# Turning two query tiles per stick-breaking head without TensorE, with weights as differences for B and a late division for A

## The chip, the cores and the metric

The kernel runs on one core of one Trainium2 chip. The metric is the device time of one execution in microseconds (us). The time before the change is 806.25 us, the median of 3 runs (804.82 to 810.35).

## The reference

One encoder layer over 1024 prompt rows and 32 sample rows of width 1024, in float32. Two groups of eight heads read the same normalised input: A is a softmax attention in a band with a clipped relative bias, B is stick-breaking attention (each key takes its share of what the later keys have left over). Both results are gated, projected, normalised and added, and a per-layer embedding is gated in.

```python
u = rmsnorm(h, g_pre) @ w_in
qa, ka, va, ga, qb, kb, vb, gb = jnp.split(u, SPLIT_IDX, axis=-1)
...
def band_attention(q, k, v, q_pos, k_pos, bias_table):
    s = jnp.einsum('bqhd,bkhd->bhqk', q, k).astype(jnp.float32) * ATTN_SCALE
    ...
    s = s + bias_table[:, rel].astype(jnp.float32)[None]
    ...
    s = jnp.where(ok[None, None], s, NEG_INF)
    w = jax.nn.softmax(s, axis=-1).astype(v.dtype)
    return jnp.einsum('bhqk,bkhd->bqhd', w, v)
...
def stick_breaking(q, k, v, q_pos, k_pos):
    z = jnp.einsum('bqhd,bkhd->bhqk', q, k).astype(jnp.float32) * ATTN_SCALE
    causal = (k_pos[None, :] < q_pos[:, None])[None, None]
    log_beta = jax.nn.log_sigmoid(z)
    log_1m = jnp.where(causal, jax.nn.log_sigmoid(-z), 0.0)
    after = lax.cumsum(log_1m, axis=3, reverse=True) - log_1m
    w = jnp.where(causal, jnp.exp(log_beta + after), 0.0).astype(v.dtype)
    return jnp.einsum('bhqk,bkhd->bqhd', w, v)
```

Then y = concat(oA * silu(gA), oB * silu(gB)) @ w_out, h + RMSNorm(y), and the embedding with its gate h @ w_ple_gate.

## The kernel before

**How it is written down.** Every operation is recorded by a planner (`Recorder`, from line 264). Each gets a cost from a table of assumed durations (`cost`, lines 338 to 369) and a key, and `order` (372 to 437) simulates the five engines and the one DMA queue with them and fixes the program that each engine runs, in order: PE (TensorE), DVE (VectorE), ACT (ScalarE), POOL (GpSimd) and SP (SyncE, which issues the DMAs). All instructions are issued at line 450, so rows of the profile all say L450 and are told apart by the names of their tiles. On PE the operations of attention go ahead of the dense products where both are ready; the two are woven at 1252 to 1276. If one cost or one operation changes, the whole order is made anew.

**Numbers.** Products run in fp32r, with each operand split in a part that fp32r holds (`...h`, written by an ACT cast) and the rest (`...l`, by a DVE or POOL subtract): hi x hi, hi x lo and lo x hi are added in PSUM.

**Stages.** First the input rows are normalised and the first products made. Then come eight units, A0, B0, A1, B1, A2, B2, A3, B3 (line 1184), each a pair of heads. Beside the attention of a unit PE makes the dense products of the next unit's q, k and v columns (`col_steps`, from 712: tiles `mm_qA`, `mm_kB` and so on, each chunk of 352 rows 24 matmuls in four parts). Unit 7 has no next one; beside it run all eight gate products, `mm_gA` and `mm_gB`. A gate chunk is the product, a sigmoid on ACT, a multiply on DVE, and a multiply on POOL with the attention result read back from DRAM (tiles `sggA`, `oggA`; scratch `o_dr`); it is stored to `og_dr`. The last two B gates wait for the last attention step. After attention its pools are closed (1407), the output weights come in four rounds (`woB_0` to `woB_3` and `woT_0` to `woT_3`, two raw buffers, tag "ao"), ACT and DVE split them, PE makes the embedding products (`ple`), then the products of the output (`o0P` first; operands `oB` and `A11o`, the first block of gated rows), and of the embedding's gate.

**One head.** Eight query tiles of 128 rows. `begin` (784) loads A's bias. `scores(i)` (813 to 852) makes the scores `SA_i_j` or `SB_i_j` in PSUM, in two halves j where there are over 512 columns. A's tile has up to 5 blocks of 128 keys, B's tile i has i + 1.
- A: DVE adds the bias and takes the row maximum, negates it; ACT takes the exponential with the row sum; DVE takes the reciprocal; POOL scales the tile of weights. The small columns are `statA`.
- B: DVE adds the mask to the diagonal block; ACT writes sigmoid(-z) to `om` and sigmoid(z) to `be`; DVE scans the products of sigmoid(-z) from the right; POOL multiplies the two.

The weights stand in `be`, a ring of 3384 columns, the scratch of scan and bias in `om`, a ring of 3076 (line 514). `weights_t(i)` (860 to 903) turns the tile so that keys are on partitions, into the rings `wTh` and `wTl`. It has two ways. Most tiles go through PE: transposes `ptwA` or `ptwB`, up to four blocks to a PSUM bank, then an ACT cast and a DVE subtract. Tiles named in `ROUND` (line 31: 4 and 6 of A's heads, none of B's) go around PE: DVE turns every 32 x 32 square into `om`, one DMA stores that to a scratch in DRAM (`swapA`), four DMAs bring it back in the right places of `be`, and the ACT cast and the DVE subtract read it there (lines 870 to 895). `values(g)` (910 to 927) makes the products with v for four query tiles, `PVA_g` or `PVB_g`; `otB` is its result on the way to `o_dr`. Both `weights_t` and `values` are put two steps behind the scores (`LAG_T`, `LAG_V`).

Of the kernel before, what the change touches and what calls it, by code (L numbers as in the profile page):

```python
# [30 lines left out]
ROUND = {"A": ((4,),(6,)), "B": ()}  # L31
# [424 lines left out]
def stream_step(  # L456
# [22 lines left out]
    o_dr = [scratch([P, T], f"o_dr{n}") for n in range(8)]  # L479
    og_dr = scratch([8, P, T], "og_dr")  # L480
# [33 lines left out]
    ring0, ring1 = Arena(rec, at, "om", 3076), Arena(rec, at, "be", 3384)  # L514
# [11 lines left out]
    NAMES = ["qA", "kA", "vA", "gA", "qB", "kB", "vB", "gB"]  # L526

# [78 lines left out]
    def bias_rows():  # L606

        rb = ring0.tile([8, 257], "rb")
        dma(rb, rel_bias[0])
        R = ring1.tile([8, 768], "R")  # L610
        nc.gpsimd.memset(R, 0.0)
        nc.vector.tensor_scalar(R[:, 256:768], R[:, 256:768], rb[:, 0:1], None, ALU.add)
        nc.vector.tensor_copy(R[:, 0:256], rb[:, 0:256][:, ::-1])
        dma(r_dr, R)
# [97 lines left out]
    def col_steps(j):  # L712
# [7 lines left out]
        def mms(c, part):  # L720
# [20 lines left out]
            if k == "g":  # L741
# [36 lines left out]
    def attention(ab, p, h):  # L778
# [5 lines left out]
        def begin():  # L784
            if ab == "A":
                bias = at2.tile([P, 640], F32, tag="bias", name=f"bias{nm}", bufs=2)
                dma(bias, bias_src(2 * p + h, P, 0, 640))
                nc.gpsimd.memset(bias[0:HD, 0:HD], NEG)
                nc.gpsimd.memset(bias[HD:P, 576:640], NEG)
                box["bias"] = bias  # L790

# [21 lines left out]
        def scores(i):  # L813
# [14 lines left out]
            if ab == "B":  # L828
# [6 lines left out]
                for a, b, s in pieces:  # L835
                    nc.scalar.activation(w1[:, a:b], s, AF.Sigmoid)
                for a, b, s in reversed(pieces):
                    rev = w0[:, a + 1:b + 1][:, ::-1]
                    nc.vector.tensor_tensor_scan(rev, rev, s, 1.0 if b == n else w0[:, b + 1:b + 2], ALU.mult, ALU.bypass)
                nc.gpsimd.tensor_tensor(w1[:, 0:n], w1[:, 0:n], w0[:, 1:n + 1], ALU.mult)  # L840
            else:
                m = small.tile([P, 4], F32, tag="stat", name=f"stat{nm}_{i}", bufs=6)
                for j, (a, b, s) in enumerate(pieces):
                    nc.vector.tensor_tensor_reduce(
                        w0[:, a:b], s, box["bias"][:, n - b:n - a][:, ::-1], 1.0,
                        -3e38 if j == 0 else m[:, j - 1:j], ALU.add, ALU.max, m[:, j:j + 1])
                last = len(pieces) - 1
                nc.vector.tensor_scalar(m[:, 2:3], m[:, last:last + 1], -1.0, None, ALU.mult)
# [1002 lines left out]
```

## Time and profile before

| | |
|---|---|
| median of 3 runs | 806.25 us (804.82 to 810.35) |
| span of the profiled execution | 802.6 us; the page gives no other time of that execution |
| granted TensorE clock | 0.999 |
| instructions | PE 4734 matmuls, DVE 1129, ACT 1163, POOL 554 |
| TensorE's waits for other engines, over 0.1 us | 4.9 us in 8 rows |
| DMA | 145.39 MB in the main queue, 61.3% of its engines' time |

The span runs from the first instruction to the last. A row of an operation reads: line, engine, operation, output and inputs by tile name, shape, count, busy time, mean ns of one, and the idle time of that engine just before it with what ended it. A matmul's own duration is longer than the time it holds up the next one, since they are pipelined.

### The profile page before, as it was taken

To read this page: it belongs to the slowest core of one execution; us is meant where nothing else is said; L and a number is where in the kernel's file an instruction comes from. 1 tells how busy PE (TensorE), PEld (TensorE's weight loads), DVE (VectorE), ACT (ScalarE), POOL (GpSimd) and SP (SyncE) were. 2 spreads that over 40 slices of the span, in tenths; PEclk is the share of its full clock that TensorE was granted. 3 is DMA by queue.
4 is the path that set the end of the run, shared out by engine and by line. 5 is a ranking of instruction groups with operands and counts; after the bars stand their busy time and mean duration, and the time that the engine had idled before them with its cause. 6 is when DMAs were issued, how large, how long until landed. Compare 5 with 4: busy or idle time off the path is not lost.

```text
span 802.6 us, 14554 instructions
## 1 busy us (share of the span) xinstructions
PE 792.0 (99%) x4734; PEld 731.4 (91%) x4734; DVE 565.7 (70%) x1129; ACT 539.5 (67%) x1163; POOL 469.5 (58%) x554
## 2 busy tenths in 40 slices
PE   9999999999999999999999999999999999999997
PEld 7899999999999999999999899999998877888786
DVE  7627878777787888776787586854554786587655
ACT  6636787786586777776787577644437868876741
POOL 6625867795686866635473265554553448599613
PEclk9999999999999999999999999999999999999999
DMA  9419986538876565833325656344389957769634
GB/s 293 135 46 285 236 230 186 153 112 254 220 229 198 145 184 158 208 103 102 92 60 141 146 158 205 99 149 138 105 277 300 288 174 242 236 197 345 215 117 131
DMA packets 147390, 146.32 MB, mean 182 GB/s; under 512 B 37409, under 2 KB 109257, under 8 KB 147314
## 3 DMA queue, kind: packets, MB, share of 16 engines
q1 hardware_dynamic: 147314, 145.39, 61.3%
q8 instruction: 38, 0.62, 0.3%
q14 instruction: 38, 0.31, 0.1%
HBM read 90.78 MB, written 46.16 MB: 171 GB/s over the span
## 4 chain that ended last, share of the span: by engine, by line
PE 89%; DVE 3%; DMA 2%; POOL 2%; ACT 1%; issue 1%; SPq 1%; POOLq 0%; DVEq 0%; ACTq 0%
PE mm_gB L450 6%; PE mm_gA L450 6%; PE mm_kB L450 6%; PE mm_qB L450 6%; PE mm_qA L450 5%; PE mm_kA L450 5%; PE mm_vB L450 4%; PE PVB L450 4%; PE mm_vA L450 4%; PE SB L450 4%; PE ptwB L450 4%; PE SA L450 3%; PE PVA L450 3%; PE g0P L450 2%; PE g1P L450 2%; PE o1P L450 2%
## 5 line engine op out<-in xcount | busy, mean ns | idle before, releaser
L450 POOL TENSOR_TENSOR be<-be,om 128x512 f32<-128x512 f32 (+8 forms) x66 | 82.9, 1260 | 77.8 <-DVE om L450 43.9
L450 DVE TENSOR_TENSOR_SCAN om<-om,SB 128x384 f32<-128x384 f32 (+5 forms) x96 | 92.6, 968 | 21.9 <-ACT be L450 11.7
L450 POOL TENSOR_SCALAR be<-be,statA 128x640 f32<-128x640 f32 (+3 forms) x64 | 44.4, 698 | 44.4 <-DVE statA L450 35.8
L450 DVE TENSOR_TENSOR wTl<-ptwB,wTh 128x512 fp32r<-128x512 f32 (+3 forms) x96 | 50.8, 546 | 13.8 <-ACT wTh L450 12.4
L450 ACT ACTIVATE om<-SB 128x384 f32<-128x384 f32 (+5 forms) x96 | 47.4, 499 | 19.0 <-DVE SB L450 14.2
L450 ACT CAST wTh<-ptwB 128x512 fp32r<-128x512 f32 (+3 forms) x96 | 44.6, 483 | 14.5 <-PE ptwB L450 10.5
L450 ACT ACTIVATE be<-om,statA 128x640 f32<-128x640 f32 (+3 forms) x64 | 44.6, 698 | 11.2 <-DVE statA L450 9.6
L450 ACT ACTIVATE be<-SB 128x384 f32<-128x384 f32 (+5 forms) x96 | 46.8, 498 | 6.8 <-DVE om L450 6.3
L450 PE MATMUL ptwB<-ident,be 128*128 128x128 f32 x288 | 44.0, 273 | 0.1
L450 PEld LDWEIGHTS ptwB<-ident,be 128*128 128x128 f32 x288 | 34.9, 140 | 2.2 <-PE mm_vA L450 0.4
L450 DVE CUSTOM_DVE_ANT_0 om<-SA,biasA 128x320 f32<-128x320 f32 (+2 forms) x64 | 30.7, 480 | 5.3 <-PE SA L450 4.9
L450 PE MATMUL SB<-kdB,LB 128*128 128x384 f32 (+5 forms) x96 | 34.0, 357 | 0.3 <-DVE om L450 0.3
L450 ACT CAST wTh<-ptwA 128x512 fp32r<-128x512 f32 (+2 forms) x64 | 26.0, 429 | 12.0 <-PE ptwA L450 11.4
L450 DVE TENSOR_TENSOR wTl<-ptwA,wTh 128x512 fp32r<-128x512 f32 (+2 forms) x64 | 29.7, 482 | 4.9 <-ACT wTh L450 4.0
L450 PE MATMUL SB<-klB,LB 128*128 128x384 f32 (+5 forms) x96 | 32.9, 347 | 0.0
L450 PE MATMUL SA<-kdA,LA 128*128 128x320 f32 (+2 forms) x96 | 30.0, 319 | 1.1 <-DVE LA L450 0.8
L450 PE MATMUL SA<-klA,LA 128*128 128x320 f32 (+2 forms) x96 | 29.8, 319 | 0.0
L450 POOL TENSOR_TENSOR gB<-gB,gB 128x256 f32<-128x256 f32 x32 | 26.6, 848 | 0.7 <-DMA gB<-in_w_ple_gate_dram 0.4
L450 PE MATMUL ptwA<-ident,be 128*128 128x128 f32 x160 | 26.5, 274 | 0.0
L450 DVE TENSOR_TENSOR SB<-SB,maskb 128x128 f32<-128x128 f32 x64 | 18.0, 292 | 9.9 <-PE SB L450 8.0
L450 POOL TENSOR_TENSOR oB<-oB,oB 128x256 f32<-128x256 f32 x32 | 23.6, 754 | 1.4 <-DMA oB<-in_w_out_dram 1.3
L450 POOL TENSOR_TENSOR h<-h,x 128x512 f32<-128x512 f32 (+1 forms) x18 | 23.0, 1295 | 0.8 <-DVE h L450 0.8
(706 smaller groups left out, 2668.3 us busy)
## 6 DMA issues: line engine op xcount, KB each, us to landing
swapA<-om SPq DMA_DIRECT2D x16, 320.0 KB, 3.5
be<-swapA SPq DMA_DIRECT2D x64, 80.0 KB, 2.9
oB<-in_w_out_dram SPq DMA_DIRECT2D x16, 256.0 KB, 3.9
sum_dro<-oB SPq DMA_DIRECT2D x16, 256.0 KB, 2.9
gB<-in_w_ple_gate_dram SPq DMA_DIRECT2D x16, 256.0 KB, 3.7
sum_drg<-gB SPq DMA_DIRECT2D x16, 256.0 KB, 3.2
x<-in_x_prompt_dram SPq DMA_DIRECT2D x16, 256.0 KB, 4.1
h_dr<-h SPq DMA_DIRECT2D x8, 512.0 KB, 3.6
```

The costliest lines, as they stand in the source:

```text
L450: getattr(getattr(tc.nc, o.what[0]), o.what[1])(*args, **kw)
```

## The change

Three things are done together.

1. `ROUND` names tiles 4 and 6 of B's heads too, so these go through DVE squares and DRAM. That takes 96 `ptwB` transposes off PE, with 32 ACT casts and 32 DVE subtracts of up to 512 columns behind them, and puts in 16 DVE turns, 16 stores `swapB`, 64 loads, and 16 casts and 16 subtracts of 640 and 896 columns.
2. B's weights become differences. With r(j) the product of sigmoid(-z) over the keys from j on, the weight of key j is r(j + 1) - r(j). So the second sigmoid goes (96 ACT instructions), the scan runs in place, and POOL subtracts where it multiplied.
3. A divides late. Its weights stay unscaled; the sums of a head's eight tiles go to one tile `sums`, whose reciprocals (one per head) PE transposes and a DMA stores to `rs_dr`. Each A gate chunk reads those rows back, spread over 64 partitions by two DMAs, and POOL multiplies once more with them. 64 POOL scalings of up to 640 columns go and 12 multiplies of 352 come; 64 small DVE reciprocals become 8. The scores are made negative (query scale, bias, mask and the row minimum in place of the maximum), so that the 64 small DVE negations go too.

The ring `be` shrinks from 3384 to 3328 columns. In all PE has 4646 matmuls in place of 4734, SP issues 781 DMAs in place of 668, and ACT loads its function table 12 times in place of 8.

```diff
-ROUND = {"A": ((4,),(6,)), "B": ()}
+ROUND = {"A": ((4,),(6,)), "B": ((4,),(6,))}
...
+    rs_dr = scratch([8, T], "rs_dr")
...
-    ring0, ring1 = Arena(rec, at, "om", 3076), Arena(rec, at, "be", 3384)
+    ring0, ring1 = Arena(rec, at, "om", 3076), Arena(rec, at, "be", 3328)
...
+    def fixed_columns():
+        x = small.tile([8, NS], F32, tag="fixed", name="fixed")
+        nc.gpsimd.memset(x, 1.0)
+        dma(rs_dr[:, SEQ:T], x)
...
-                box["og"] = at2.tile([P, CH], F32, tag="bias", name=f"og{kind}{p}_{c}", bufs=2)
-                dma(box["og"], o_dr[n][:, cs])
+                box["og"] = at2.tile([P, 2, CH], F32, tag="stg", name=f"og{kind}{p}_{c}", bufs=3)
+                dma(box["og"][:, 0], o_dr[n][:, cs])
+                if ab == "A":
+                    for h in range(2):
+                        row = rs_dr.real[2 * p + h:2 * p + h + 1, cs]
+                        dma(box["og"][h * HD:(h + 1) * HD, 1], Raw(rs_dr, bass.AP(tensor=row.tensor, offset=row.offset, ap=[[0, HD], [1, CH]])))
...
-                nc.gpsimd.tensor_tensor(sg, sg, box["og"], ALU.mult)
+                nc.gpsimd.tensor_tensor(sg, sg, box["og"][:, 0], ALU.mult)
+                if ab == "A":
+                    nc.gpsimd.tensor_tensor(sg, sg, box["og"][:, 1], ALU.mult)
...
-                nc.scalar.activation(box["st"][:, cs], acc, AF.Copy, scale=SCALE)
+                nc.scalar.activation(box["st"][:, cs], acc, AF.Copy, scale=-SCALE if ab == "A" else SCALE)
...
+                box["sums"] = small.tile([P, 8], F32, tag="sums", name=f"sums{nm}", bufs=2)
...
-                for a, b, s in pieces:
-                    nc.scalar.activation(w1[:, a:b], s, AF.Sigmoid)
                 for a, b, s in reversed(pieces):
-                    rev = w0[:, a + 1:b + 1][:, ::-1]
-                    nc.vector.tensor_tensor_scan(rev, rev, s, 1.0 if b == n else w0[:, b + 1:b + 2], ALU.mult, ALU.bypass)
-                nc.gpsimd.tensor_tensor(w1[:, 0:n], w1[:, 0:n], w0[:, 1:n + 1], ALU.mult)
+                    rev = w0[:, a:b][:, ::-1]
+                    nc.vector.tensor_tensor_scan(rev, rev, s, w0[:, b:b + 1], ALU.mult, ALU.bypass)
+                nc.gpsimd.tensor_tensor(w1[:, 0:n], w0[:, 1:n + 1], w0[:, 0:n], ALU.subtract)
...
-                nc.vector.tensor_scalar(m[:, 2:3], m[:, last:last + 1], -1.0, None, ALU.mult)
-                nc.scalar.activation(w1[:, 0:n], w0[:, 0:n], AF.Exp, bias=m[:, 2:3], accum_out=m[:, 3:4])
-                nc.vector.reciprocal(m[:, 3:4], m[:, 3:4])
-                nc.gpsimd.tensor_scalar(w1[:, 0:n], w1[:, 0:n], m[:, 3:4], 1.0, ALU.mult, ALU.mult)
+                nc.scalar.activation(w1[:, 0:n], w0[:, 0:n], AF.Exp, bias=m[:, last:last + 1], scale=-1.0, accum_out=sums[:, i:i + 1])
+                if i == 7:
+                    nc.vector.reciprocal(sums, sums)
+                    pt = psum("T", f"pts{nm}")
+                    nc.tensor.transpose(pt[0:8, 0:P], sums, ident)
+                    row = at.tile([P, 4 * P], F32, tag="ot", name=f"sumrow{nm}", bufs=2)[0:8, 0:P]
+                    nc.scalar.copy(row, pt[0:8, 0:P])
+                    dma(rs_dr[2 * p + h, 0:SEQ].rearrange("(i q) -> i q", q=P), row)
```

How it moves instructions is seen best in the first B head. On PE, before, the transposes of tile 6 stand between the dense products of q (a number behind a name is one buffer of that name):

```order
L450 MATMUL SB_3_0_1905<-kdB_1302,LB_1306 128x512
L450 MATMUL SB_3_0_1905<-klB_1305,LB_1306 128x512
L450 MATMUL mm_qA_0_1795<-hnl_126,wh_qA_0_1613 128x352
L450 MATMUL mm_qA_0_1795<-hnl_126,wh_qA_1_1624 128x352 x4
L450 MATMUL ptwB_6_0_1923<-ident,be 128x128 x4
L450 MATMUL ptwB_6_4_1928<-ident,be 128x128 x3
L450 MATMUL mm_qA_1_1857<-hnh_124,wh_qA_0_1613 128x352 x4
```

After the change PE's program at the scores of tile 3 of the next head reads so; the transposes of tile 6 are gone, and dense products have moved together:

```order
L450 MATMUL SB_3_0_1834<-kdB_1262,LB_1266 128x512
L450 MATMUL SB_3_0_1834<-klB_1265,LB_1266 128x512
L450 MATMUL mm_kA_2_1737<-hnl_145,wh_kA_1_1337 128x352 x4
L450 MATMUL mm_qA_0_1799<-hnh_140,wh_qA_0_1602 128x352 x4
L450 MATMUL mm_qA_0_1799<-hnh_140,wh_qA_1_1615 128x352
L450 MATMUL SB_4_0_1864<-kdB_1262,LB_1266 128x320
L450 MATMUL SB_4_0_1864<-klB_1265,LB_1266 128x320
```

Further on PE the product with v of this head's last four tiles stands before:

```order
L450 MATMUL mm_qA_1_1857<-hnl_127,wh_qA_0_1613 128x352 x4
L450 MATMUL SB_4_1_1996<-kdB_1302,LB_1306 128x320
L450 MATMUL SB_4_1_1996<-klB_1305,LB_1306 128x320
L450 MATMUL mm_qA_1_1857<-hnl_127,wh_qA_1_1624 128x352
L450 MATMUL PVB_1_1893<-wTh,v2B_1417 128x512 x4
L450 MATMUL SB_5_0_2009<-kdB_1302,LB_1306 128x384
L450 MATMUL SB_5_0_2009<-klB_1305,LB_1306 128x384
```

and after. It needs the turned tile 6, now out of `be` and not out of PSUM; the number of matmuls since tile 6's scores (`SB_6_1_1699`) is 138:

```order
L450 MATMUL SB_5_0_1955<-klB_1265,LB_1266 128x384
L450 MATMUL mm_qA_1_1886<-hnh_141,wl_qA_1_1595 128x352 x2
L450 MATMUL mm_qA_1_1886<-hnl_144,wh_qA_0_1602 128x352 x4
L450 MATMUL mm_qA_1_1886<-hnl_144,wh_qA_1_1615 128x352 x4
L450 MATMUL PVB_1_1881<-wTh,v2B_1408 128x512 x4
L450 MATMUL SB_5_1_1983<-kdB_1262,LB_1266 128x384
L450 MATMUL SB_5_1_1983<-klB_1265,LB_1266 128x384
```

On DVE, before, tile 6 is two subtracts out of PSUM, which stand among the masks and scans of the next head:

```order
L450 TENSOR_TENSOR wTl<-ptwB_5_4_1900,wTh 128x256
L450 TENSOR_TENSOR SB_1_0_1841<-SB_1_0_1841,maskb 128x128
L450 TENSOR_TENSOR SB_2_0_1845<-SB_2_0_1845,maskb 128x128
L450 TENSOR_TENSOR SB_3_0_1905<-SB_3_0_1905,maskb 128x128
L450 TENSOR_TENSOR wTl<-ptwB_6_0_1923,wTh 128x512
L450 TENSOR_TENSOR wTl<-ptwB_6_4_1928,wTh 128x384
L450 SCALAR_TENSOR_TENSOR om<-om,SB_1_0_1841 128x256
L450 SCALAR_TENSOR_TENSOR om<-om,SB_2_0_1845 128x384
L450 SCALAR_TENSOR_TENSOR om<-om,SB_3_0_1905 128x512
L450 TENSOR_TENSOR wTl<-ptwB_7_0_1974,wTh 128x512
```

After the change DVE turns tile 6 (the first row) and goes on with other work:

```order
L450 STREAM_TRANSPOSE om<-be 128x7x4x32
L450 SCALAR_TENSOR_TENSOR om<-om,SB_7_1_1754 128x512
L450 SCALAR_TENSOR_TENSOR om<-om,SB_7_0_1700 128x512
L450 TENSOR_TENSOR v2B_1408<-vtB_1386,v2B_1408 128x8x64
L450 SCALAR_TENSOR_TENSOR om<-om,SB_0_0_1755 128x128
L450 TENSOR_TENSOR SB_1_0_1820<-SB_1_0_1820,maskb 128x128
L450 TENSOR_TENSOR SB_2_0_1821<-SB_2_0_1821,maskb 128x128
L450 TENSOR_TENSOR v2B_1687<-vtB_1386,v2B_1687 128x8x64
L450 SCALAR_TENSOR_TENSOR om<-om,SB_1_0_1820 128x256
L450 TENSOR_TENSOR SB_3_0_1834<-SB_3_0_1834,maskb 128x128
L450 TENSOR_TENSOR otB_0_1583<-PVB_0_1707,otB_0_1583 64x512
```

and the subtract of tile 6 is the last but one row of what follows; 20 instructions lie between the turn and the subtract:

```order
L450 TENSOR_TENSOR wTl<-ptwB_5_0_1679,wTh 128x512
L450 TENSOR_TENSOR wTl<-ptwB_5_4_1715,wTh 128x256
L450 STREAM_TRANSPOSE ktA_1711<-stkA_1348 128x512
L450 TENSOR_TENSOR wTl<-be,wTh 128x4x5x32
L450 SCALAR_TENSOR_TENSOR om<-om,SB_2_0_1821 128x384
L450 TENSOR_TENSOR wTl<-ptwB_7_0_1898,wTh 128x512
L450 SCALAR_TENSOR_TENSOR om<-om,SB_3_0_1834 128x512
L450 TENSOR_TENSOR SB_4_1_1931<-SB_4_1_1931,maskb 128x128
L450 SCALAR_TENSOR_TENSOR om<-om,SB_4_1_1931 128x320
L450 SCALAR_TENSOR_TENSOR om<-om,SB_4_0_1864 128x320
L450 TENSOR_TENSOR wTl<-be,wTh 128x4x7x32
L450 TENSOR_TENSOR SB_5_1_1983<-SB_5_1_1983,maskb 128x128
```

On SP, before, the same stretch holds loads and stores of weight sums and of finished rows:

```order
L450 DMA oB_1764<-in_w_out_dram 128x512
L450 DMA oB_1772<-in_w_out_dram 128x512
L450 DMA out_dram<-vtB_1382 128x8x128
L450 DMA sum_dro<-oB_1764 128x512
L450 DMA oB_1836<-in_w_out_dram 128x512
L450 DMA kdA_1793<-kdA_1793 64x1024
L450 DMA o_dr_67<-otB_0_1595 64x512
L450 DMA oB_1907<-in_w_out_dram 128x512
L450 DMA klA_1797<-klA_1797 64x1024
L450 DMA out_dram<-ktA_1730 32x16x32 x4
```

After the change the stores and loads of the squares stand among them, tile 6's last load behind the store of `otB_0`:

```order
L450 DMA be<-swapB_4_104 32x4x160 x2
L450 DMA oB_1760<-in_w_out_dram 128x512
L450 DMA oB_1761<-in_w_out_dram 128x512
L450 DMA be<-swapB_4_104 32x4x160 x2
L450 DMA swapB_6_105<-om 128x896
L450 DMA oB_1804<-in_w_out_dram 128x512
L450 DMA out_dram<-vtB_1386 128x8x128
L450 DMA be<-swapB_6_105 32x4x224 x3
L450 DMA o_dr_67<-otB_0_1583 64x512
L450 DMA sum_dro<-oB_1761 128x512
L450 DMA be<-swapB_6_105 32x4x224
```

Where attention ends, ACT before splits the last round of output weights and casts the first block of gated rows, `A11o`, with several `ple` copies still to come:

```order
L450 CAST oB_7524<-woB_3_7772 128x512
L450 CAST oB_7525<-woB_3_7772 128x512
L450 COPY ple_1_7754<-ple_1_7822 128x512
L450 CAST php_6519<-ptp_7466 128x2x32
L450 CAST A11o_7863<-uo_6588 128x512
L450 CAST oT_7527<-woT_3_7810 128x512
L450 COPY ple_0_7661<-ple_0_7832 128x512
L450 CAST oT_7526<-woT_3_7810 128x512
L450 COPY ple_1_7818<-ple_1_7841 128x512
```

After the change all but one of the `ple` copies are ahead of it, and the last round of weights comes right before it:

```order
L450 COPY xA11o_7626<-uo_7540 128x512
L450 CAST whA11o_7392<-uo_7540 128x512
L450 CAST oB_7359<-woB_3_7598 128x512
L450 CAST oB_7360<-woB_3_7598 128x512
L450 COPY ple_0_7677<-ple_0_7634 32x512
L450 CAST A11o_7683<-uo_6367 128x512
L450 CAST oT_7362<-woT_3_7623 128x512
L450 COPY xA12o_7694<-uo_6367 128x512
```

More of the change, by code (lines that the diff above doesn't have):

```diff
@@ L611, in bias_rows @@
         nc.gpsimd.memset(R, 0.0)
-        nc.vector.tensor_scalar(R[:, 256:768], R[:, 256:768], rb[:, 0:1], None, ALU.add)
-        nc.vector.tensor_copy(R[:, 0:256], rb[:, 0:256][:, ::-1])
+        nc.vector.tensor_scalar(R[:, 256:768], R[:, 256:768], rb[:, 0:1], None, ALU.subtract)
+        nc.vector.tensor_scalar(R[:, 0:256], rb[:, 0:256][:, ::-1], -1.0, None, ALU.mult)
         dma(r_dr, R)
@@ L1017, in scores @@
                         w0[:, a0:b0], s, bx["bias"][:, NK - b0:NK - a0][:, ::-1], 1.0,
-                        -3e38 if j == 0 else m[:, 0:1], ALU.add, ALU.max, m[:, j:j + 1])
-                nc.vector.tensor_scalar(m[:, 2:3], m[:, 1:2], -1.0, None, ALU.mult)
-                nc.scalar.activation(w1[:, 0:NK], w0[:, 0:NK], AF.Exp, bias=m[:, 2:3], accum_out=m[:, 3:4])
+                        3e38 if j == 0 else m[:, 0:1], ALU.add, ALU.min, m[:, j:j + 1])
+                nc.scalar.activation(w1[:, 0:NK], w0[:, 0:NK], AF.Exp, bias=m[:, 1:2], scale=-1.0, accum_out=m[:, 3:4])
                 nc.vector.reciprocal(m[:, 3:4], m[:, 3:4])
```

8 lines of the change are left out of this document (5 added, 3 removed).

## The prediction

> **What bounds the kernel now.** I read the page's busy line and chain first, then the busy time by stretches, then the waits of TensorE (PE).
>
> ```profile
> PE 792.0 (99%) x4734; PEld 731.4 (91%) x4734; DVE 565.7 (70%) x1129; ACT 539.5 (67%) x1163; POOL 469.5 (58%) x554
> ...
> PE 89%; DVE 3%; DMA 2%; POOL 2%; ACT 1%; issue 1%; SPq 1%; POOLq 0%; DVEq 0%; ACTq 0%
> ```
>
> PE is busy in 792.0 of 802.6 us and holds 89% of the chain. The stretches say whether that is so where the change works: from about 70 to 576 us, the attention.
>
> ```profile
> 40.00:600.00 560.00, 557.59 (x3611) 540.05 (x3610) 404.48 (x874) 377.61 (x839) 332.65 (x402) 1.00 0.59 165
> ...
> 120.00:130.00 10.00, 10.00 (x67) 9.63 (x66) 8.96 (x12) 7.58 (x18) 9.18 (x13) 1.00 0.57 185
> ...
> 300.00:390.00 90.00, 90.00 (x585) 87.67 (x585) 70.15 (x163) 68.08 (x147) 51.93 (x67) 1.00 0.56 148
> ```
>
> The columns are length, then busy time of PE, PEld, DVE, ACT and POOL, the granted clock, the DMA share and GB/s. Between 40 and 600 us PE idles for 2.4 us of 560, at a clock of 1.00, with 557.59 / 3611 = 0.154 us for a matmul. Over 90 us of that VectorE (DVE) is at 78%; over ten of them at 90%. So PE work that goes here shortens the kernel one for one, work saved on the others does nothing by itself, and the engine that could take over is DVE.
>
> ```profile
> PE idle L450 <- DVE newh L450: 1.3, 1, 1.3
> ...
> PE SA L450 <- DVE LA L450: 0.8, 1, 0.8
> ...
> PE SB L450 <- DVE om L450: 0.3, 1, 0.3
> PE PVA L450 <- ACT wTh L450: 0.2, 1, 0.2
> ```
>
> Of these waits the last two are the whole price that A's existing turned tiles and a full score ring have today: 0.5 us.
>
> **The change part by part.** *The PE transposes of B.* Tile 4 has 5 blocks and tile 6 has 7, so 12 of a head's 36 transposes go, 96 in all.
>
> ```profile
> L450 PE MATMUL ptwB<-ident,be 128*128 128x128 f32 x288 | 44.0, 273 | 0.1
> ...
> 127.20 1.05 PE L450 MATMUL ptwB<-ident,be 128*128 128x128 f32 x8
> ```
>
> The first row gives 273 ns from start to end of one, but matmuls overlap. The second row, eight in one block that lasts 1.05 us, shows what one holds up the next by: (1.05 - 0.273) / 7 = 0.111 us. The busy column gives 44.0 / 288 = 0.153, which has latency in it wherever a short run ends. I take 0.111: 96 x 0.111 = 10.7 us gone, with 96 x 0.153 = 14.7 as the far end. A's late division adds one transpose of the row sums per head, 8 x 0.111 = 0.9. Net: -9.8 us. The Trainium skill ("TensorE: Matmul & The Clock Gate", Part 4: PE-mode transpose) gives about 275 ns for a transpose inside a kernel; as a latency it agrees with the 273 of the row, as a price the block of eight speaks against it, and by it the sum would be about 24 us instead of 9.8.
>
> *The way that takes their place.* A's tiles 4 and 6 have gone it all along:
>
> ```profile
> L450 DVE STREAM_TRANSPOSE om<-be 128x640 f32<-128x640 f32 x16 | 13.4, 838 | 3.1 <-POOL be L450 3.1
> ...
> L450 ACT CAST wTh<-be 128x640 fp32r<-128x640 f32 x16 | 11.6, 727 | 0.7 <-DMA be<-swapA 0.6
> ...
> L450 DVE TENSOR_TENSOR wTl<-be,wTh 128x640 fp32r<-128x640 f32 x16 | 18.1, 1131 | 4.6 <-ACT wTh L450 4.2
> ...
> swapA<-om SPq DMA_DIRECT2D x16, 320.0 KB, 3.5
> be<-swapA SPq DMA_DIRECT2D x64, 80.0 KB, 2.9
> ```
>
> The last column of the DMA rows is the time from issue to landing. B's tile 6 has 896 columns, 1.4 times 640. Along the path after its scores, from these rows and the next: the diagonal mask 0.29, a sigmoid 0.55, two scans 2.22, the POOL subtract 1.77, the turn 0.838 x 1.4 = 1.17, the store 3.5, four loads about 4.2 (three further issues of some 0.4, then 2.9), the cast 0.727 x 1.4 = 1.02, the subtract 1.131 x 1.4 = 1.58: 16.3 us without queues.
>
> ```profile
> L450 DVE TENSOR_TENSOR_SCAN om<-om,SB 128x448 f32<-128x448 f32 x16 | 17.8, 1112 | 4.5 <-ACT be L450 2.2 <-ACT om L450 2.0
> ...
> L450 POOL TENSOR_TENSOR be<-be,om 128x896 f32<-128x896 f32 x8 | 14.2, 1773 | 15.2 <-DVE om L450 12.5 <-ACT Kh0sA L450 1.9 <-ACT be L450 0.8
> ...
> L450 DVE TENSOR_TENSOR SB<-SB,maskb 128x128 f32<-128x128 f32 x64 | 18.0, 292 | 9.9 <-PE SB L450 8.0 <-PE ptwB L450 1.4
> ...
> L450 DVE TENSOR_TENSOR wTl<-ptwB,wTh 128x512 fp32r<-128x512 f32 x48 | 32.4, 681 | 12.1 <-ACT wTh L450 11.1 <-PE PVB L450 0.6
> ...
> L450 ACT ACTIVATE om<-SB 128x448 f32<-128x448 f32 x16 | 8.8, 551 | 6.1 <-DVE SB L450 3.4 <-PE SB L450 2.3 <-POOL be L450 0.3
> ```
>
> What time has it? In the changed order of the first B head, 138 matmuls stand between the last scores of tile 6 and PVB_1's first product: 138 x 0.154 = 21.3 us; the shortest of the eight heads has 133, the others 151 to 283. The 5 us left are for queues. The store and loads share SP's queue: the fourth load of tile 6 is behind the store of otB_0, which waits for the PVB_0 products, so everything behind that store waits with it. On DVE 20 instructions stand between the turn of tile 6 and its subtract: eight scans (about 7.5 us by the scan groups, 512 columns at 1.24), four masks 1.17, four splits 2.6 and four others 2.6 (estimated at 0.65 each, near the split of 512 columns), 13.9 us. The turn cannot begin before the masks of SB_7_1 and the next head's SB_0_0, which stand 31 matmuls (4.8 us) after the scores. So 4.8 + 0.3 + 1.2 + 13.9 + 1.6 = 21.8 us, and the subtract is wanted eight matmuls after the first product, at 22.5. It fits with 0.7 us to spare: tight, in the engine that is nearest to full. Bounds: nothing, if it always fits (or a gain of the 0.5 us that the two waits above cost); 8 heads x 1.1 = 9 us, if each subtract of tile 6 takes its worst.
>
> ```profile
> L450 DVE TENSOR_TENSOR wTl<-be,wTh x16: 800/826/2494, 94.2 to 488.5; 128x640 fp32r<-128x640 f32 x16
> ```
>
> This is its minimum, median and maximum; 2.494 is 1.7 above the median, less the 0.7 to spare gives about 1.1. I take +0.5, as much again as A's sixteen turned tiles cost now, since A's row is the same mechanism; A had a little more room (158 to 200 matmuls in the five heads where this can be counted alike). The Trainium skill ("SBUF — State Buffer", SBUF: two separate sides) says that a VectorE operation with two SBUF inputs and a GpSimd operation that reads SBUF lock each other out for a whole instruction; the spread 800 to 2494 agrees, and the new subtract, which reads `be` in place of PSUM, puts B's tiles under that rule too.
>
> *Work off PE.*
>
> ```profile
> L450 ACT ACTIVATE be<-SB 128x384 f32<-128x384 f32 (+5 forms) x96 | 46.8, 498 | 6.8 <-DVE om L450 6.3
> ...
> L450 POOL TENSOR_SCALAR be<-be,statA 128x640 f32<-128x640 f32 (+3 forms) x64 | 44.4, 698 | 44.4 <-DVE statA L450 35.8
> ...
> L450 POOL TENSOR_TENSOR sggA<-sggA,oggA 128x352 f32<-128x352 f32 x12 | 11.5, 960 | 11.0 <-DVE sggA L450 9.7 <-issue 1.3
> ...
> L450 DVE RECIPROCAL statA<-statA 128x1 f32<-128x1 f32 x64 | 9.7, 155 | 3.8 <-ACT be L450 3.3
> ...
> L450 DVE TENSOR_SCALAR statA<-statA 128x1 f32<-128x1 f32 x64 | 9.5, 149 | 1.2
> ```
>
> ACT loses the second sigmoids, -46.8; POOL the normalisations, -44.4, and gains 11.5; DVE loses 9.7 + 9.5 in A's units and gains 8 x (0.84 + 1.17) = 16 for the turns in B's, so it is even overall and some 2 us a head fuller where it is fullest. B's subtract on POOL in place of the multiply is the same shape and costs nothing. SP issues 113 more DMAs, and the 12.6 MB of B's squares (12 blocks of 64 KB, out and back, eight heads) raise the queue's 145 MB by 9%. All this costs and brings nothing as long as PE does not wait: it lies beside the 557.59 us. If that cover goes, the price is that of the DVE queue above.
>
> *The end of attention.* PE's dense work of the last unit is spread differently: between the last PVB_0 and the first `o` product now stand 197 matmuls, before 247, so 50 x 0.154 = 7.7 us less cover for loading and splitting the output weights.
>
> ```profile
> 575.07 0.80 PE L450 MATMUL PVB<-wTl,v2B 128*128 128x512 f32 x4
> ...
> 618.30 0.40 PE L450 MATMUL ple<-wph0False,php 128*64 128x512 f32 x1
> ...
> 619.23 1.08 PE L450 MATMUL o0P<-oB,A11o 128*128 128x512 f32 x4
> ```
> ```profile
> 612.72 0.62 ACT L450 CAST A11o<-uo 128x512 fp32r<-128x512 f32 x1
> ```
> ```profile
> 613.37 0.69 DVE L450 TENSOR_TENSOR A11o<-xA11o,A11o 128x512 fp32r<-128x512 f32 x1 [0.54 <-ACT A11o L450]
> ```
>
> A11o was ready at 614.06, 38.2 us after PVB_0's end (575.87), and used at 619.23, 43.4 after it. With 7.7 less it is used at 35.7: 2.5 us late if nothing else moved (upper bound), none if the weights start as much earlier as the order of SP allows. In ACT's order, though, the cast of A11o now stands behind the copy of the next to last PLE group. That group ends where the last begins, at 618.30 in the row above, so copy 0.2 + cast 0.62 + subtract 0.69 follow it while PE has 0.93 us left: +0.6, with a hand-over +0.7, which I take.
>
> **The sum.** 802.6 - 10.7 + 0.9 + 0.5 + 0.7 = 794.0 us of span. The median of the runs, 806.25, stands 3.65 above the profiled span (which is all that the page gives of that execution); with it 797.6 us, 8.6 less or -1.1%. A measurement of this kernel can tell about 1% (8.1 us, so 798.2) from no change: the forecast lies just beyond it.
>
> **The rivals.**
> 1. The turned tiles come late. Place: PVB_1 of each B head, or the ring that its tiles hold longer. For it: 0.7 us to spare on DVE, 90% busy there. Against: A's tiles cost 0.2 us. It decides at 0.7 us of delay per head; 1.2 us of wait in each of the 8 heads eats the whole gain, so 0.5 to 1.5 us gives 801 to 809. It ends slower by 1% where each head waits 2.2 us more (17.9 / 8), which is four DMA landings taking 3 us longer together: 815.
> 2. The end is late by 3 to 6 us, because the last weight round now waits for the last gate store: 600 to 620 us would show PE idle, and the time is 800 to 803.
> 3. PE gains more: at 0.153 us a transpose 88 x 0.153 = 13.5, and with no new wait 806.25 - 13.5 = 792.8. By the 0.273 of the group row as a full price, as the page's rule above would have it, 88 x 0.273 = 24.0 gives 783.5. The block of eight speaks against that.
> 4. Nothing moves, because PE is not the bound: 806. Only where DVE sets the pace in all B units; the 90.00 of 90.00 row speaks against it.
>
> **How the numbers follow.** My forecast, 795.5 to 800: 0.55, of which 0.37 lies below 798.2. Rival 3: 0.15 (0.02 of it the full latency). Rivals 1 and 4 without a loss over 1%: 0.15, with one: 0.08. Rival 2: 0.07. Faster by over 1%: 0.37 + 0.15 = 0.52; within 1%: 0.18 + 0.15 + 0.07 = 0.40; slower: 0.08. The range reaches from rival 3's 793 to 804.5, beyond which rival 1 keeps about 0.13; on the low side 0.04 is left out.
>
> **What would show it.** PE with 4646 matmuls and some 10 us less busy time, its idle time still under 13 us; no row of PE waiting for wTl or wTh in PVB over 1 us in total; one short wait ahead of the o products; POOL and ACT 30 to 45 us less busy. I am wrong if PVB, SB or the transposes left in B wait for DVE by more than a few us, or if PE's busy time falls by much more or less than 10.

## The result and the profile after

The changed kernel takes 807.28 us (median of 20 runs, 806.2 to 809.1), the kernel before 806.27 (20 runs); the ratio is 0.9996 (95% interval 0.9981 to 1.001). That is no change, where 797.6 was forecast. The profiled execution has a span of 806.5 us (before: 802.6). The 20 times of the kernel before lie in two groups, eleven from 804.8 to 806.3 us and nine from 809.1 to 811.1, and by its span its profiled execution is one of the quick ones, so that the two profiles are 3.9 us apart where the medians are 1.0 apart.

The page of the changed kernel, and its time by stretches (length, then busy PE, PEld, DVE, ACT, POOL, granted clock, DMA share, GB/s):

```profile
PE 784.5 (97%) x4646; PEld 722.4 (90%) x4646; DVE 575.5 (71%) x1007; ACT 507.8 (63%) x1063; POOL 436.8 (54%) x503
...
PE 84%; ACT 5%; POOL 3%; DVE 3%; DMA 2%; issue 2%; SPq 1%; DVEq 0%; ACTq 0%; POOLq 0%
```
```profile
0.00:40.00 40.00, 35.51 (x204) 30.89 (x205) 27.41 (x43) 24.91 (x49) 24.18 (x47) 1.00 0.66 215
40.00:600.00 560.00, 550.46 (x3529) 531.84 (x3528) 411.81 (x748) 344.38 (x736) 300.91 (x351) 1.00 0.67 190
600.00:806.50 206.50, 198.55 (x917) 159.62 (x915) 136.25 (x217) 138.50 (x280) 111.71 (x106) 0.98 0.69 224
```

The first and last of these stretches in the kernel before:

```profile
0.00:40.00 40.00, 36.97 (x210) 32.79 (x211) 28.38 (x44) 25.26 (x49) 24.51 (x46) 1.00 0.68 215
...
600.00:802.60 202.60, 197.49 (x917) 158.58 (x915) 132.88 (x212) 136.58 (x275) 112.31 (x107) 1.00 0.69 224
```

TensorE (PE) is busy for 7.5 us less, and idle for 11.4 us more: 22.0 in place of 10.6. Of the idle time 7.1 us are new between 40 and 600 us (9.5 in place of 2.4), 2.8 after 600, 1.5 in the first 40. PE's share of the chain falls from 89 to 84%, and ACT appears in it with 5%. In the waits of PE eight rows of 4.9 us in total have become sixteen; the first of them:

```profile
PE o0P L450 <- ACT A11o L450: 2.5, 1, 2.5
PE ptx L450 <- DVE be L450: 2.2, 2, 1.3
PE SB L450 <- DVE om L450: 1.9, 3, 1.1
PE mm_kB L450 <- ACT stvA L450: 1.5, 1, 1.5
PE PVA L450 <- ACT wTh L450: 1.3, 1, 1.3
PE ptwA L450 <- ACT be L450: 1.3, 1, 1.3
PE idle L450 <- DVE newh L450: 1.3, 1, 1.3
PE ptsA L450 <- DVE sumsA L450: 1.0, 2, 0.9
```

No PVB is among them: PE did not stand still for B's turned tiles. It did for other things, most of them once, for 0.9 to 2.5 us in total each.

**Behind table loads.** Four of these waits stand right behind a load of ScalarE's function table. Two of the places in the timeline of the changed kernel (start, duration, operation, and in brackets the idle time before it):

```profile
235.97 1.28 ACT L450 ACT_TABLE_LOAD   x1
...
237.27 0.83 ACT L450 ACTIVATE be<-om,statA 128x640 f32<-128x640 f32 x1
...
238.22 0.20 DVE L450 RECIPROCAL sumsA<-sumsA 128x8 f32<-128x8 f32 x1 [1.29 <-ACT be L450]
...
238.48 0.27 PE L450 MATMUL ptsA<-ident,sumsA 128*8 128x128 f32 x1 [0.86 <-DVE sumsA L450]
```
```profile
305.94 1.28 ACT L450 ACT_TABLE_LOAD   x1
...
307.23 0.40 ACT L450 ACTIVATE be<-om,statA 128x128 f32<-128x128 f32 x1
...
307.63 0.43 ACT L450 COPY stvA<-mm_vA 128x352 f32<-128x352 f32 x1
...
308.12 0.43 PE L450 MATMUL mm_kB<-hnh,wh_kB 128*128 128x352 f32 x1 [1.55 <-ACT stvA L450]
```

In the first an exponential of A is asked for between sigmoids of B, and the transpose of the row sums waits for it. In the second the copy that frees a PSUM bank stands behind the load, and the next dense product waits for the bank. The other two are SB at 243.19 us (1.10, behind the load at 240.61) and ptwA at 473.83 (1.31, behind the load at 470.75). Together 0.86 + 1.55 + 1.10 + 1.31 = 4.8 us. A load is not among the costs that the planner knows (lines 338 to 369), so its order leaves no room for one. At two edges, A1 to B1 and A3 to B3, it mixes the last exponentials of the A unit with the first sigmoids of the B unit; that makes two loads more at each. Three of the four waits, 3.3 us, stand behind loads at these two edges. The fourth, 1.55 us, stands behind the one load from B1 to A2, which the kernel before makes too (at 301.81 us) without a wait of PE behind it.

**At the end of attention.** The scores of the last head's tile 4 are made at 541 us. From the timeline of the changed kernel:

```profile
541.05 0.31 PE L450 MATMUL SB<-klB,LB 128*128 128x320 f32 x1
...
559.02 2.67 POOL L450 TENSOR_TENSOR be<-om 128x640 f32<-128x640 f32 x2 [1.16 <-DVE Vl2sB L450]
...
560.30 0.85 DVE L450 STREAM_TRANSPOSE om<-be 128x640 f32<-128x640 f32 x1 [0.37 <-POOL be L450]
...
561.21 0.45 SPq L450 DMA_DIRECT2D swapB<-om  x1
...
567.52 1.82 SPq L450 DMA_DIRECT2D be<-swapB  x4
...
574.20 1.61 DVE L450 TENSOR_TENSOR wTl<-be,wTh 128x640 fp32r<-128x640 f32 x1
...
588.79 0.88 SPq L450 DMA_DIRECT2D woB<-in_w_out_dram  x2
...
621.89 0.99 PE L450 MATMUL o0P<-oB,A11o 128*128 128x512 f32 x2 [2.50 <-ACT A11o L450]
```

POOL writes the tile only at 559, after gate work and a wait of 1.16 us for the sample attention. The store goes out at 561.2, the loads at 567.5, behind a gate's store in SP's queue, and the subtract ends at 575.8: 34 us after the scores. PVB_1, which needs this tile, begins at 575.3 (before: 567.1). PVB_0 stands behind it and ends at 583.9 (before: 575.9). The first output weights are issued at 588.8 (before: 582.9), their last round at 611.6 (before: 604.9), and the first output product waits 2.5 us. What follows is slower too:

```profile
620.00:622.00 2.00, 0.10 (x1) 0.11 (x1) 1.91 (x4) 1.66 (x4) 0.08 (x1) 1.00 1.08 376
622.00:624.00 2.00, 2.00 (x6) 1.55 (x7) 2.00 (x3) 1.88 (x4) 1.92 (x2) 0.55 1.12 363
624.00:626.00 2.00, 2.00 (x7) 1.60 (x6) 2.00 (x2) 1.05 (x2) 0.91 (x1) 0.60 1.16 314
626.00:628.00 2.00, 2.00 (x11) 1.61 (x10) 0.75 (x2) 1.12 (x3) 1.75 (x2) 1.00 1.15 309
```

For four microseconds behind the wait the granted clock is 0.55 and 0.60: 2 x 0.45 + 2 x 0.40 = 1.7 us lost while PE counts as busy. So the 3.9 us between the two profiles are 9.2 us of PE work saved (7.5 + 1.7) against 1.7 lost at half clock and 11.4 of idle time.

### The profile page after: what moved, and what is told of

Same layout as the page of the kernel before. It is cut to its first block, busy times and chain, and to the rows that moved or that the text cites. A ratio compares the mean times of both kernels' runs of the same rounds, so it can differ in the third digit from the quotient of the medians.

```text
span 806.5 us, 14268 instructions
## 1 busy us (share of the span) xinstructions
PE 784.5 (97%) x4646; PEld 722.4 (90%) x4646; DVE 575.5 (71%) x1007; ACT 507.8 (63%) x1063; POOL 436.8 (54%) x503
## 4 chain that ended last, share of the span: by engine, by line
PE 84%; ACT 5%; POOL 3%; DVE 3%; DMA 2%; issue 2%; SPq 1%; DVEq 0%; ACTq 0%; POOLq 0%
PE mm_gB L450 6%; PE mm_gA L450 6%; PE mm_qA L450 5%; PE mm_kA L450 5%; PE mm_vA L450 5%; PE mm_qB L450 4%; PE mm_kB L450 4%; PE SB L450 4%; PE PVB L450 4%; PE mm_vB L450 3%; PE PVA L450 3%; PE SA L450 3%; PE ptwB L450 3%; PE o0P L450 3%; PE o1P L450 2%; PE g0P L450 2%
## 5 line engine op out<-in xcount | busy, mean ns | idle before, releaser
L450 DVE TENSOR_TENSOR_SCAN om<-om,SB 128x384 f32<-128x384 f32 (+5 forms) x96 | 95.6, 1005 | 12.1 <-ACT om L450 9.8
L450 POOL TENSOR_TENSOR be<-om 128x128 f32<-128x128 f32 (+7 forms) x64 | 77.5, 1216 | 49.4 <-DVE om L450 23.1
L450 ACT CAST wTh<-ptwB 128x512 fp32r<-128x512 f32 (+3 forms) x64 | 29.4, 482 | 21.1 <-PE ptwB L450 16.2
L450 DVE TENSOR_TENSOR wTl<-be,wTh 128x640 fp32r<-128x640 f32 (+1 forms) x32 | 35.5, 1108 | 7.1 <-ACT wTh L450 6.8
L450 DVE TENSOR_TENSOR wTl<-ptwB,wTh 128x512 fp32r<-128x512 f32 (+3 forms) x64 | 33.5, 545 | 7.7 <-ACT wTh L450 4.6
L450 DVE CUSTOM_DVE_ANT_0 om<-SA,biasA 128x320 f32<-128x320 f32 (+3 forms) x64 | 30.0, 483 | 6.2 <-PE SA L450 5.8
L450 DVE STREAM_TRANSPOSE om<-be 128x640 f32<-128x640 f32 (+1 forms) x32 | 28.8, 900 | 4.7 <-ACT be L450 2.3
L450 POOL TENSOR_TENSOR sggA<-sggA,oggA 128x352 f32<-128x352 f32 x24 | 23.9, 997 | 13.6 <-DVE sggA L450 10.2
L450 PE MATMUL ptwB<-ident,be 128*128 128x128 f32 x192 | 29.3, 273 | 0.0
L450 ACT CAST wTh<-be 128x640 fp32r<-128x640 f32 (+1 forms) x32 | 24.9, 779 | 6.4 <-DMA be<-swapA 3.8
```

The costliest lines, as they stand in the source:

```text
L450: getattr(getattr(tc.nc, o.what[0]), o.what[1])(*args, **kw)
```

## The experiments

Theory 1: the saving on PE is real, and single waits of the new order take it back. Theory 2: the way through DVE and DRAM costs it. Theory 3: any new order has some 10 us of waits, whatever is changed. Every edit makes the whole order anew, so a run changes more than the wait that it is aimed at. Each ratio is to executions of the kernel before that ran beside the kernel in question; their medians were 806.3 us beside the changed kernel, 809.6 beside after_table, turn_alone, late_alone and no_turn, 806.5 beside after_last, after_table_last, late_table and diff_alone, and 806.0 beside the rest. So the ratio is not the quotient of two rows.

| kernel | matmuls | table loads | median us | ratio to before (95%) |
|---|---|---|---|---|
| changed | 4646 | 12 | 807.28 | 0.9996 (0.9981 to 1.001) |
| after_table | 4646 | 8 | 806.49 | 0.998 (0.9958 to 1.0003) |
| after_last | 4658 | 12 | 807.93 | 0.9998 (0.9978 to 1.0019) |
| after_table_last | 4658 | 8 | 804.38 | 0.9964 (0.9941 to 0.9987) |
| atl_pool | 4658 | 8 | 800.16 | 0.9922 (0.9899 to 0.9944) |
| turn_alone | 4638 | 14 | 818.73 | 1.0127 (1.0099 to 1.0155) |
| turn_table_last | 4650 | 8 | 807.47 | 1.0025 (1.0005 to 1.0044) |
| late_alone | 4742 | 14 | 819.26 | 1.0132 (1.0105 to 1.0158) |
| late_table | 4742 | 8 | 817.28 | 1.012 (1.0094 to 1.0146) |
| diff_alone | 4734 | 10 | 812.17 | 1.0067 (1.0048 to 1.0086) |
| no_turn | 4742 | 10 | 813.38 | 1.0055 (1.0037 to 1.0073) |
| tdl_pool | 4650 | 8 | 806.45 | 1.0002 (0.9991 to 1.0014) |
| before_pool | 4734 | 8 | 806.05 | 0.9998 (0.9987 to 1.0009) |

**Eight table loads (after_table).** A chain in the planner, and a price for the change of table:

```diff
+        now_t, last_t, run_t = None, [], []
+        for o in self.ops:
+            t = next((a for a in o.args if a is AF.Exp or a is AF.Sigmoid), None) if o.eng == "ACT" else None
+            if t is None:
+                continue
+            if t is not now_t:
+                now_t, last_t, run_t = t, run_t, []
+                o.busy += 1283
+            o.after.update(last_t)
+            run_t.append(o)
```

> The changed kernel with one thing more: the planner keeps the exponentials and the sigmoids of ScalarE in the order in which they are recorded, so that they do not mix at the edges of units, and charges 1283 ns for each change of table. The program then loads the table 8 times, as the kernel before, in place of 12. Theory 1 (the 9.8 us of TensorE work are saved, and are taken back by single waits that the new order brings; four of them, 0.9 + 1.1 + 1.6 + 1.3 = 4.8 us, stand right behind a table load of 1.28 us that the planner does not know of): these four go, the other waits may move, 801 to 804 us, ratio to the kernel before 0.994 to 0.998. Theory 2 (the way through DVE and DRAM is itself what costs, through DVE and the DMA queues): table loads are beside the point, 806 to 808 us. Theory 3 (the order is a matter of chance, any new order costs some 10 us of waits): anywhere from 800 to 812 with other waits of 10 to 15 us in total.

The time is 806.49, above that range. The stretch that the theory speaks of did what it said:

```profile
40.00:600.00 560.00, 555.18 (x3557) 536.28 (x3557) 408.59 (x750) 340.47 (x734) 301.21 (x351) 1.00 0.67 191
```

PE's idle time there falls from 9.5 to 4.8 us, the 4.7 that were asked for, and the last gate product ends at 600.2 in place of 605.5. But the last round of output weights came no sooner (issued at 612.6 us, in the changed kernel at 611.6):

```profile
619.46 1.52 PE L460 MATMUL o1P<-oB,whA11o 128*128 128x512 f32 x2 [3.24 <-ACT oB L460]
...
622.21 1.22 PE L460 MATMUL o0P<-oB,A11o 128*128 128x512 f32 x2 [0.80 <-ACT A11o L460]
```

PE reaches the output products 3 us too early and loses 2.4 us at half clock behind that. A wait was removed, and the next bound took the gain.

**The last head not turned (after_last, after_table_last).**

```diff
-        together = {i: g for g in ROUND[ab] for i in g}
+        together = {} if (ab, p, h) == ("B", 3, 1) else {i: g for g in ROUND[ab] for i in g}
```

> The changed kernel, but the very last head of B turns tiles 4 and 6 through TensorE; 4658 matmuls, 12 table loads as in the changed kernel. In its order 238 matmuls stand between the last PVB_0 and the first output product, in the changed kernel 197 (before: 247). Theory 1 (the wait for A11o at the end, 2.5 us, and the half clock behind it, 1.7 us, come from the last head's turned tile 4, whose long way moves the end of attention towards the output products): both go, 12 transposes at 0.11 come back, 1.3 us; 2.9 us less than the changed kernel, 803.5 to 805.5. Theory 2 (the loads of the output weights are late for another reason): the wait ahead of the output products stays, 806.5 to 809 us.

> The changed kernel with both: 8 table loads by the planner's chain of exponentials and sigmoids, and the last head of B not turned. 4658 matmuls, 246 between the last PVB_0 and the output products. Theory 1: of the run with 8 loads alone the waits at the output products go (3.2 + 0.8 + 0.8 us) and the half clock behind them (about 2.4), 1.3 us of transposes come back: 6 us less than that run, about 800 us (798 to 802.5), ratio to the kernel before 0.990 to 0.996: faster than both kernels. Theory 3 (every new order has its own 10 us of waits): 804 to 808 us, with new waits elsewhere.

In both the wait at the output products is gone, and PVB_0 ends at 578.4 and 572.0 in place of 583.9 and 582.2. That settles the end of attention: it was the last head's turned tiles (4 and 6 together; no run parts them). The times still fell short, 807.93 and 804.38, in the ranges of the other theories: in both profiles a wait came up at g0P, 120 us after the output products began. In the timeline of after_table_last, DVE, then PE:

```profile
725.74 8.10 DVE L460 TENSOR_TENSOR gT<-raw,gT 128x512 fp32r<-128x512 f32 x1
```
```profile
735.98 4.12 PE L460 MATMUL g0P<-gT,S1g 128*128 128x512 f32 x10 [2.56 <-DVE uu L460]
```

This subtract takes 8.10 us (1.7 and 1.8 in the profile of the kernel before), and meanwhile POOL works without a pause:

```profile
724.48 2.54 POOL L460 TENSOR_TENSOR ug<-ug,s 128x512 f32<-128x512 f32 x2
726.99 1.30 POOL L460 TENSOR_TENSOR gT<-raw,gT 128x512 fp32r<-128x512 f32 x1
728.25 1.29 POOL L460 TENSOR_TENSOR gB<-raw,gB 128x512 fp32r<-128x512 f32 x1
729.50 1.29 POOL L460 TENSOR_TENSOR cc2P<-cc2P,hh 128x512 f32<-128x512 f32 x1
730.76 2.54 POOL L460 TENSOR_TENSOR gB<-raw,gB 128x512 fp32r<-128x512 f32 x2
```

It ends when POOL pauses at 733.3. The code there is untouched by the change; the next two runs ask whether it is a matter of chance.

**Without such a subtract on DVE (before_pool, atl_pool).**

```diff
-            split_slice(b, kt, raw, nc.scalar, nc.vector if count[0] % 3 == 0 else nc.gpsimd)
+            split_slice(b, kt, raw, nc.scalar, nc.gpsimd)
```

> The kernel before with one engine changed: the low halves of the late weight blocks (gT, gB, oT, oB out of raw) are all subtracted by GpSimd, where every third was VectorE's. In the profile of the run with 8 loads and the last head unturned, one such VectorE subtract took 8.10 us in place of 0.68 while GpSimd worked without a pause from 714 to 733 us; TensorE then waited 2.6 us for uu and ran at half clock behind it, 1.7 us lost. Theory 1 (that single lock is a matter of which engine comes first, and strikes the kernel before too in some executions): without the operation the kernel before shows no execution above 808 us, median 804 to 807. Theory 2 (the spread of the kernel before has another cause): its executions go on reaching 810.

The executions of before_pool lie between 805.4 and 807.5, those of the kernel before, beside it, between 804.6 and 810.4. Three of those 29 are above 808, so few that twelve executions can miss them by chance. More weighs that none of the 30 executions of before_pool, atl_pool and tdl_pool, which have no such subtract on DVE, is more than 2.7 us above the fastest of its kernel, while turn_table_last, which has it, has five of twelve above 809 in the same round. That fits a lock that strikes the kernel before too, in some executions; no profile of that kernel shows it. Its median is not moved here (806.05 against 805.97).

> The changed kernel with 8 table loads, the last head of B unturned, and the low halves of the late weight blocks all on GpSimd. Theory 1: the wait of 2.6 us at g0P and the half clock behind it (1.7) go: 799 to 802 us, ratio 0.990 to 0.995, faster than both kernels. Theory 3 (a new order brings other waits of that size): 803 to 808.

800.16 us, as expected: 0.8% faster than the kernel before (0.9922, 0.9899 to 0.9944). Its waits of PE begin:

```profile
PE SA L460 <- DVE statA L460: 1.5, 1, 1.5
PE idle L460 <- DVE newh L460: 1.3, 1, 1.3
PE ptx L460 <- DVE be L460: 1.0, 2, 0.8
PE ple L460 <- ACT wph0True L460: 1.0, 1, 1.0
```

No wait behind a table load, at the output products or at g0P is left. The engine change does not make the difference by itself: before_pool has it too and takes 806.05.

**The parts by themselves.** Each is the kernel before with one or two of the three parts, some with the edits above as well; no_turn, late_alone and late_table also keep the ring of 3328 columns.

> The kernel before with the first part alone: tiles 4 and 6 of B's heads turned by DVE and DRAM; the weights of B are still products of two sigmoids and A still divides early. 4638 matmuls, 14 table loads. Theory 1: PE's busy time falls by about 10.7 us, and six more table loads of 1.28 us take back up to 7.7 of it if each is waited for: 799 to 804 us, with waits behind table loads. Theory 2: DVE is fuller here than in the changed kernel (the small reciprocals and negations are still there), so PE waits for DVE in SB, ptwB or PVB by more than 8 us in total: 806 to 812 us.

> The first part alone, with 8 table loads in place of 14 and the last head unturned; 4650 matmuls. Theory 1 (most of the 819 us of the first part alone are waits behind table loads and at the end): 17 us of waits before the end of attention fall to under 9, the 3.7 us at the output products go: 801 to 807. Theory 2 (without the relief of the other two parts VectorE and ScalarE are too full in B's units): the waits for om, statA, wh and wl stay, 810 to 818.

turn_alone is slower by 1.3%, above the ranges of both theories; PE waits in 25 rows. PE is busy for 792.0 us, as long as in the kernel before, which has 96 transposes more; some 3.3 us of that are lost at half clock, and the rest is not explained. With 8 loads and the last head unturned it takes 807.47, just above Theory 1's range: about 1% came from these two things (the ratio falls from 1.0127 to 1.0025), but the 9 us that PE was spared are still not seen. What is left is in single waits on ACT and DVE (11.5 us of PE's waits, in the kernel before 4.9); some of the largest:

```profile
PE mm_vA L460 <- ACT wh_vA L460: 1.3, 1, 1.3
...
PE ptkA L460 <- DVE wTl L460: 1.3, 1, 1.3
PE mm_kA L460 <- ACT wh_kA L460: 1.2, 1, 1.2
PE SB L460 <- DVE om L460: 1.2, 1, 1.2
```

That fits a share of Theory 2: DVE is busy for 583.4 us in this run and for 574.1 in after_table_last, which has the other two parts as well.

> As the run before it but without the late division: first and second part alone, 8 table loads, the last head unturned, low halves on GpSimd. 4650 matmuls. Theory 1: eight transposes (0.9 to 1.2 us) less on TensorE and 33 us more on GpSimd beside it: 798 to 802. Theory 2 (VectorE and GpSimd hold TensorE up; the late division is what pays for the turns): 804 to 810, with waits for VectorE and GpSimd.

806.45, in Theory 2's range. The same kernel with the late division (atl_pool) is 6.3 us faster, though PE has eight transposes more. DVE and POOL have 19 and 30 us more to do without it (573.7 and 481.7 against 555.1 and 452.0 busy). That this is the reason is not shown: against atl_pool PE waits 2.5 us longer for ACT, 1.6 for POOL and 0.1 for DVE, and loses 1.4 more at half clock. These are single waits again, which Theory 3 would also have.

> The kernel before with the third part alone: A divides late. 4742 matmuls, 14 table loads. Theory 1: 0.9 us more on PE and six more table loads, up to 7.7 us of waits: 808 to 814 us. Theory 2 (table loads cost nothing, since ACT is at two thirds): within 1.5 us of the kernel before, 805 to 808 us.

> The late division of A alone, now with 8 table loads in place of 14. Theory 1: the wait of 3.5 us behind four loads in a row at 470 to 476 us goes, and the half clock that follows it (8 us at half speed for part, 3.3 us): about 7.5 us less than 819, 810 to 813 us. Theory 2 (table loads cost nothing, the late division itself does): 817 to 820 us.

Alone, the late division is slower by 1.3%. Four loads in a row, from 469.6 to 477.4 us, made PE wait 3.5 us, with 2.7 us lost at half clock after it. With 8 loads that wait goes, but the time falls by 2 us and not by 7.5: this order has a wait of 2.8 us for a load of the sample attention (SsA for QsA, at 217 us) with a half clock behind it, and the lock at g0P. Theory 1 was right on the cause of one wait and wrong on the sum. The number lies in Theory 2's range, the waits are such as Theory 3 expects; the run does not part the two.

> The kernel before with the second part alone: B's weights as differences, no second sigmoid. 4734 matmuls as before, 10 table loads. Theory 1: PE's work is unchanged and ScalarE's 47 us were not on the path; two more loads cost 0 to 2.6 us: 805 to 810 us, ratio 0.999 to 1.004. Theory 2 (ScalarE's and GpSimd's queues do hold PE up): below 803 us.

> The changed kernel without its first part: B's tiles 4 and 6 go through TensorE again; differences for B and late division for A stay. 4742 matmuls, 10 table loads. Theory 1: PE busy time about 0.9 us above the kernel before and two more table loads, 1 to 3 us: 807 to 811 us, slower than the kernel before by 0.1 to 0.6%. Theory 2: no turned B tiles, so few waits, and ACT and POOL have 40 us less to do each: 804 to 807 us.

812.17 and 813.38, both slower by some 0.6% and above the ranges of both theories, though ACT has 33 us less to do in the one and 32 in the other. diff_alone has the same wait of 2.8 us at SsA and 1.5 at half clock; no_turn has the lock at g0P (2.6 us and 1.7 at half clock).

## Why the prediction was wrong

- *PE bounds the kernel, and what is saved there counts one for one.* Half right. PE's work fell by nearly what was forecast, but a span is PE's busy time and its idle time together, and the idle time did not stay. Of the working's own signs this is the one that failed: 22.0 us idle, where under 13 were forecast.
- *96 transposes at 0.111, less 0.9 for the row sums: -9.8.* Right in this kernel: 7.5 us less busy and 1.7 at half clock make 9.2. The price of 0.153 or 0.273 each (rival 3) falls.
- *B's turned tiles come in time, with 0.7 us to spare.* Right for PVB, on which no wait is seen; in the last head the tile came 8 us later than before, and PE had gate products to fill the time. The subtract of 896 columns took 1.30 us on average, less than the 1.58 allowed.
- *"I take +0.5, as much again as A's sixteen turned tiles cost now."* This is the step that failed. Between 40 and 600 us 7.1 us of idle time are new: 4.8 behind table loads, 1.1 more at A's own PVA (1.3 in place of 0.2), and small ones. The working asked what the moved work waits for, and not what the whole new order waits for. The count of loads, 12 for 8, stood in the description of the change, and at 1.28 us each was never put in the sum.
- *"All this costs and brings nothing as long as PE does not wait."* The condition did not hold. The order before was one in which PE waited 2.4 us of 560; a new one does not inherit that. Of the thirteen kernels here the one with the order of before but for one engine (before_pool) has 2.7 there, the others 3.8 to 14.4. Beside that, DVE, said to come out even, was busy 9.8 us longer (565.7 to 575.5).
- *The end of attention, +0.7.* Mis-sized: 2.5 of wait and 1.7 at half clock. The working had the right figure and set it aside: its upper bound was 2.5 us, with PE at the output products 35.7 us after PVB_0's end. PE was there after 35.5, and the cast of A11o ended 38.0 after it (before: 37.5). The weights did not start as much earlier as the choice of 0.7 needed.
- *Rival 2* (the end late by 3 to 6 us, 800 to 803) named the place, the size (4.2 us) and the order: the last round of weights, ahead of the last gate store before (604.9 and 608.2 us), is now behind it (611.6 and 607.7). Alone it would not have brought the time back to 807. *Rival 1* named DVE's fullness; no wait at PVB bears it out. *Rival 4* has the number, 806, by luck: nothing was to move there, and PE's work and waits both moved by some 10 us. (In rival 1's price 17.9 should be 16.7 by the working's own numbers; nothing hangs on it.)

So the forecast span, 794.0, was exceeded by 12.5 us: 10.2 are idle time beyond the 1.2 allowed, 1.7 the half clock, 0.6 the smaller saving.

What stays open: which of the small waits of 0.2 to 1.0 us goes with which part, and how much of Theory 3 is true. The runs show that the named waits can be taken out and that the time then falls as forecast (atl_pool); they do not show that another order of the same work would not do as well or as badly, and atl_pool is the best of thirteen. The 1.5 us in the first 40 are most likely not the change's: after_last, which differs from the changed kernel in its last head alone, idles 3.05 us there, the kernel before 3.03, and before_pool 4.11 with the order of before.

## What to carry to other kernels

Where a planner has brought the waits of the bounding engine to nothing, a change has two prices: the work that it removes there, and the new order's own waits, which come from whatever the planner does not model. In these kernels they were table loads, an engine lock and a queue that issues in order. Before summing, count such things in the new program, find the last unit of the pipeline, where no later work hides a longer way, and use the long way everywhere but there. Then judge the change by the order mended for it.

## What was not expected of the hardware

- A wait of PE can cost more than itself. Behind 2.5 us of idling the granted clock stood near half for about 3.4 us (1.7 / 0.5) and 1.7 us were lost; behind 3.5 us (late_alone) 2.7 us. The limit is not sharp: 1.55 us at 306.6 in the changed kernel cost nothing, nor did 2.59 us ahead of 751.6 in late_table, while 1.46 us at 214.7 in atl_pool gave 0.50 between 218 and 220, and in tdl_pool four waits of 0.5 to 1.0 us between 275 and 281 gave 0.50 from 280 to 286. The Trainium skill ("TensorE: Matmul & The Clock Gate", Part 1: The HAM clock gate) has the clock go to half after an idle window of about 3.4 us, in a window that runs freely; the free window fits the blurred limit, but here much shorter waits were enough. The stretches of atl_pool:

```profile
214.00:216.00 2.00, 0.65 (x4) 0.35 (x2) 1.97 (x5) 1.61 (x5) 2.00 (x3) 1.00 0.84 279
216.00:218.00 2.00, 1.84 (x8) 1.37 (x9) 2.00 (x9) 0.81 (x3) 1.92 (x2) 0.81 0.58 190
218.00:220.00 2.00, 2.00 (x9) 2.00 (x9) 1.61 (x5) 0.63 (x2) 0.00 (x0) 0.50 0.95 241
```

The stretches of late_table, with a longer wait and no fall:

```profile
750.00:752.00 2.00, 0.43 (x2) 0.42 (x3) 2.00 (x6) 0.00 (x0) 0.00 (x0) 1.00 0.68 166
752.00:754.00 2.00, 2.00 (x11) 1.57 (x10) 1.33 (x4) 0.60 (x1) 0.00 (x0) 1.00 0.99 371
```

- A DVE operation with two SBUF inputs stood for some 7.4 us beside POOL instructions that followed each other without a pause (six of 1.27 us), not only beside one of them. It ended about 0.5 us after the last of them, and took 8.0 to 8.1 us in all five profiles that have it (after_last, after_table_last, late_alone, late_table, no_turn). That POOL holds it is read from these times. The spread of single programs suggests that it is held in some executions and not in others: after_table_last took 799.7 to 808.5 us, with the lock in the profiled execution of 805.9, and atl_pool, with that subtract on POOL, 799.0 to 801.7. The Trainium skill ("SBUF — State Buffer", SBUF: two separate sides) describes the lock for one instruction; that a row of them can keep it is what these runs suggest.
- A change of ScalarE's function table took 1.28 us each time, and in late_alone four followed each other within 8 us.
